# One plain gate-and-up tile less in the last half layer, its sums of x and 1/rms at earlier places, and the new keys' and values' transpositions in two shared pairs of PSUM banks

## The chip, the cores and the metric

The kernel runs on one core of one Trainium2 chip. The metric is the device time of one execution in microseconds; the time before is 1618.53 us, the median of three runs (1618.33 to 1619.42).

## The reference: what is computed

One inference step of a two-layer decoder, for a prompt of 512 tokens and 8 single sample tokens that share all weights. All is float32, the model's width is 1024 and the channel mixer's is 2816. Each layer is two half layers of SwiGLU with a token mixer between them:

```
x += 0.5 * swiglu(rms(x));  x += mixer(rms(x));  x += 0.5 * swiglu(rms(x))
swiglu(h) = (silu(h @ wg) * (h @ wu)) @ wd
rms(x) = x * rsqrt(mean(x*x) + eps) * g
```

The first layer's mixer is a causal pooling with windows of 2 to 16. The second's is sliding-window attention with sinks, over keys and values that are projected once, from x after the first layer. The outputs are the final norm's y, the last pooling rows, and the last 128 positions of keys and values for both groups.

## The kernel before

**Data and precision.** x lies as eight tiles of 128 features by 520 tokens. Each operand is split into a high and a low part (names ending in h and l), and each product is three matmuls of 260 columns (half of the 520 tokens): high with high, low x with high weight, high x with low weight. ScalarE makes a weight's high part (`wh`, L287), VectorE its low part (`wl`, L288), four k tiles at a time: a weight piece. Six buffers of wh and wl lie between these and TensorE, so ScalarE can run some six pieces ahead. SP loads the weights into three `raw` buffers.

**The half layers.** `ffn` runs four times (fi 0 to 3; the last is the second layer's second SwiGLU). The 22 gate-and-up tiles come in parts of 8, 8 and 6, and each part ends with its product with the down weights. There are two kinds of gate-and-up tile:

- `plain_tile`: gate and up over eight k tiles, for both halves of the tokens. It takes four weight pieces in the order gate, up, gate, up, and after each it runs the next entry of a list of *hooks*. VectorE's L751 and L753 then read the gate's and the up's bank pair, with ScalarE's silu (L752) between.
- `strassen_tile`: the same result with seven products of half size, from sums of weight blocks and sums of x. It takes seven pieces. Of the sums of weights, VectorE makes two (L221, L227), POOL one inside raw (L214), and one comes from two loads into a buffer `S`, the second an accumulating one by POOL (L398). It evacuates more: ScalarE's L775, L780, L783, L791, VectorE's L787 to L798.

The first `NPL[fi]` tiles of a half layer are plain, since the sums of x and 1/rms (`R`) aren't there yet; the hooks make them. Before, `NPL` is 4, 3, 2, 3.

**Sums of x and 1/rms.** `sums` is a generator of eight steps. For each of four pairs of x tiles, ScalarE makes `xa` and `xb` (L863, two buffers in all); VectorE makes t1 (L868) and t2 (L869) in a first step, t3 (L873) and t4 (L874) in a second; each step ends with a split of its tile into th (ScalarE, L379) and tl (VectorE, L380). 1/rms is three parts: TensorE adds up the squares (L560), VectorE takes a chain of small operations (L564 to L574, then L1912), and `rstd_all` has TensorE transpose the result (L586, L587) into a bank pair from which ScalarE copies it to R (L588, L589). Each plain tile's evacuation waits for R.

**PSUM.** Outside attention the eight banks are four pairs (`duo`, names ps_ with a number). A plain tile takes one pair for the gate and one for the up half; 1/rms holds one until R is copied.

**New keys and values.** The third `ffn` begins with `outputs` among its hooks, in its first plain tile. It transposes the new keys kT and values vT from features to tokens on TensorE (L1375, L1376, L1391, L1398), ScalarE copies the banks to `win`, `knew`, `vtok` and `vnew`, and POOL's queue stores them.

**Order.** A scheduler puts the instructions of each engine in an order when the kernel is built, from the order of the code, the buffers that are free and its estimates; only operations marked `later` keep the order of the code. On the chip each engine takes its row strictly in turn.

Of the kernel before, what the change touches and what calls it, by code (L numbers as in the profile page):

```python
# [11 lines left out]
F32 = mybir.dt.float32  # L12
# [16 lines left out]
NH = 3  # L29

FIRST = 264
NPL = (4, 3, 2, 3)
PIN0 = 6
SEVEN = {(f, p) for f in range(4) for p in (0, 1)}
HD = 64
# [289 lines left out]
def yoco_step(ctx, tc, ins, outs):  # L325
# [622 lines left out]
    def deferred(n, tmp, tag, tags, lst, w=TOK):  # L948

        def f(k):  # L950
            z = pair(tags, [P, w])
            split(tuple(a[:, :TOK] for a in z), x[k], gcol(n, k))
            lst.append(z)
            square(k, tmp, tag)

        return f
# [44 lines left out]
    def start_hooks(tmp, n, tt, late, norm_tok=rstd_tok):  # L1001

        steps = sums(tmp, n, tt)
        step = lambda: next(steps, None)
        there[0] = False
        none = lambda: None

        def norm():
            norm_tok()
            step()  # L1010

        def norm_all():
            rstd_all()
            known()

        return [none] * late + [norm, step, norm_all] + [step] * 6


    mov1 = []
    with ff_pool() as tmp:  # L1020
# [131 lines left out]
                    yield  # L1152

        after = delayed(1, tmp, "g", XX, mov1, TW)
        ffn(0, tmp, mov0, start_hooks(tmp, 0, tt, 2), tt, HH, after, pool_prep(), first, hold=True)

    with tc.tile_pool(name="pm", bufs=2, reuse_waits="tile") as pm:
        for k in range(KT):
# [129 lines left out]
    with ff_pool() as tmp:  # L1288

        later(nc.sync.dma_start(pool_sample[0, :, 0:14, :], state_pool[0, :, 1:15, :]))  # L1290
        for dst, src in ((k_win_s, cache_k), (v_win_s, cache_v)):
            later(
                nc.sync.dma_start(
                    dst[:, 0:127].rearrange("b s g d -> b s (g d)"), src[:, 1:128].rearrange("b s g d -> b s (g d)")
                )
            )
        later(nc.sync.dma_start(sraw, attn_sinks.broadcast_to([P, 16])))
        for b in range(NS):
            later(nc.sync.dma_start(sink_s[b * 16 : (b + 1) * 16, 0:1], attn_sinks.rearrange("l h -> h l")))
        tt = {}  # L1300
        ffn(1, tmp, mov2, start_hooks(tmp, 2, tt, 2), tt, HH, deferred(N_KV, tmp, "g", XX, movk))


    kvp = ctx.enter_context(tc.tile_pool(name="kvp", bufs=1, space=bass.MemoryType.DRAM))
# [17 lines left out]
    with ff_pool() as tmp:  # L1322

        s4 = sinks.rearrange("p (g i b e) -> p g i b e", g=2, i=4, b=4)
        sr = sraw.rearrange("p (g e i) -> p g i e", g=2, e=2)
        for b in range(4):
            for g in range(2):
                V.tensor_copy(s4[:, g, :, b, :], sr[:, g])
        V.tensor_scalar(nsinks, sinks, -1.0, None, op0=ALU.mult)
        V.tensor_scalar(sink_s[:, 1:2], sink_s[:, 0:1], -1.0, None, op0=ALU.mult)  # L1330
        cs = rawp.tile([P, 2, TOK], F32, tag="raw", name="cs")
        nc.scalar.dma_start(cs.rearrange("p a t -> p (a t)"), consts[:, C_COS : C_COS + 2 * TOK])

        def kv_pass(after):
            banks = [duo() for _ in range(2)]
            for k0 in (0, 4):
                ws = [W.get(), W.get()]
                W.prefetch()
                for k in range(k0, k0 + 4):
                    for w, bk in zip(ws, banks):  # L1340
                        mm(w, k - k0, movk[k], bk, k == 0, k == KT - 1)
                    after(k)
            return banks

        def during_k(k):
            if k == 1:
                rstd_tok()
            if k == 3:
                rstd_all()

        mov3, tt = [], {}
        steps = sums(tmp, 3, tt)

        def during_v(k):
            mov3.append(pair(HH, [P, TOK]))
            split(mov3[k], x[k], gcol(3, k))
            if k >= 4:
                next(steps)

        kb = kv_pass(during_k)  # L1360
        for i in range(2):
            V.tensor_tensor(cs[:, i, :], cs[:, i, :], R, op=ALU.mult)
        kT = [tmp.tile([P, TOK], F32, tag="ph", name="kT", bufs=3) for g in range(2)]
        for g in range(2):
            rope(kT[g], kb[g], cs[:, 0, :], cs[:, 1, :], tmp, ("g", "t"))
        vb = kv_pass(during_v)
        vT = [tmp.tile([P, TOK], F32, tag="g", name="vT") for g in range(2)]
        for g in range(2):
            V.tensor_tensor(halves(vT[g]), vb[g][:, :, :H], halves(R), op=ALU.mult)

        def outputs():
            win = tmp.tile([P, 256], F32, tag="t", name="win")
            pk = ps()
            for g in range(2):
                T.transpose(pk[:, g * P : (g + 1) * P], kT[g][:, 384:512], ident)  # L1375
                T.transpose(pk[:NS, 256 + g * P : 256 + (g + 1) * P], kT[g][:, SP:], ident)  # L1376
            S.copy(win, pk[:, :256])
            knew = tmp.tile([NS, 256], F32, tag="sb", name="knew", bufs=2)
            vnew = tmp.tile([NS, 256], F32, tag="sb", name="vnew", bufs=2)
            S.copy(knew, pk[:NS, 256:512])  # L1380
            nc.gpsimd.dma_start(k_win_p[0].rearrange("s g d -> s (g d)"), win)
            nc.gpsimd.dma_start(k_win_s[:, 127].rearrange("b g d -> b (g d)"), knew)
            nc.gpsimd.dma_start(k_new, knew)
            for g in range(2):
                nc.gpsimd.dma_start(kT_kept[g], kT[g][:, :SP])
            for b2 in range(2):
                pv = ps()
                for b in (2 * b2, 2 * b2 + 1):
                    for g in range(2):
                        o = (b % 2) * 256 + g * P  # L1390
                        T.transpose(pv[:, o : o + P], vT[g][:, b * P : (b + 1) * P], ident)  # L1391
                vtok = tmp.tile([P, 2, 256], F32, tag="pl", name="vtok", bufs=3)
                S.copy(vtok, pv.rearrange("p (b c) -> p b c", b=2))
                nc.gpsimd.dma_start(v_kept[b2], vtok)
            nc.gpsimd.dma_start(v_win_p[0].rearrange("s g d -> s (g d)"), vtok[:, 1, :])
            pvs = ps()
            for g in range(2):
                T.transpose(pvs[:NS, g * P : (g + 1) * P], vT[g][:, SP:], ident)  # L1398
            S.copy(vnew, pvs[:NS, :256])
            nc.gpsimd.dma_start(v_win_s[:, 127].rearrange("b g d -> b (g d)"), vnew)  # L1400
            nc.gpsimd.dma_start(v_new, vnew)

        kc, kk, vv = [], [], []

        def attention_prep():


            for i in range(4):
                kc.append(splp.tile([P, 2, 256], F32, tag="S", name="kc", bufs=4))
                later(nc.sync.dma_start(kc[i], cache_k[2 * i : 2 * i + 2].rearrange("b s g d -> s b (g d)")))  # L1410
                nc.gpsimd.dma_start(kc[i][0:1], k_new[2 * i : 2 * i + 2, :])
            kept = []
            for i in range(4):
                kept.append(tmp.tile([P, SP], F32, tag="ph" if i < 2 else "pl", name="kept", bufs=3))
                src = kT_kept[i] if i < 2 else v_kept[i - 2].rearrange("p b c -> p (b c)")
                later(nc.sync.dma_start(kept[i], src))
            yield
            for i in range(4):
                z = pair(("tl", "tl"), [P, SP])
                if i < 2:  # L1420
                    kk.append(z)
                    split(z, kept[i])
                else:
                    vv.append(tuple(a.rearrange("p (b c) -> p b c", b=2) for a in z))
                    split(vv[-1], kept[i].rearrange("p (b c) -> p b c", b=2))
                if i:
                    yield
            for i in range(4):
                pk = ps()
                for j in range(4):  # L1430
                    T.transpose(pk[:, j * P : (j + 1) * P], kc[i][:, j // 2, (j % 2) * P : (j % 2 + 1) * P], ident)
                S.copy(kc[i].rearrange("p b c -> p (b c)"), pk)
                yield

        step = lambda: next(steps, None)
        hooks = [step, outputs] + [step] * 4
        ffn(2, tmp, mov3, hooks, tt, XX, deferred(4, tmp, "g", HH, mov4), attention_prep())
# [410 lines left out]
    with ff_pool() as tmp:  # L1848
# [61 lines left out]
        def norm_tok():  # L1910
            rstd_tok((0, P, 2 * P, 3 * P, 400, A.start, L.start))
            later(V.tensor_scalar(rh, r_tok[:, 5:7], -0.5, None, op0=ALU.mult))  # L1912
# [141 lines left out]
            store(3, 0)  # L2054
            ordered[0] = False

        ffn(3, tmp, mov6, start_hooks(tmp, 5, tt, 1, norm_tok), tt, HH, final_after, by_parts=tail)


# [29 lines left out]
```

## Time and profile before

| | |
|---|---|
| runs, median (lowest to highest) | 1618.53 us (1618.33 to 1619.42) |
| the profiled execution | 1619.61 us, its span 1617.8 us |
| busy of the span | PE 99%, PEld 98%, DVE 87%, ACT 60%, POOL 19% |
| granted TensorE clock | 0.997 |
| matmul records | 13350 |
| DMA | 254.64 MB, mean 157 GB/s |

Places are given in microseconds from the span's start. The transpositions of new keys and values lie at 771 to 775, the last half layer's plain tiles from 1258 to 1295. In a timeline's row stand the start, the duration, the engine, the line, the operation, output and inputs, shapes, how many were merged, and in square brackets how long the engine idled before it and what ended that. Instructions on an engine overlap, so the time that one costs in a full queue is the distance between starts and not its duration.

### The profile page before, as it was taken

The page shows a single profiled execution, that of the slowest core. Times are in us where ns is not written, and L with a number is a line of the kernel's source. Part 1 is how long each engine was busy: PE and PEld are TensorE (multiplying, and loading weights), DVE is VectorE, ACT ScalarE, POOL GpSimd, SP SyncE. Part 2 cuts the span into 40 slices and gives each one's busy share as a digit, 9 for nine tenths or more (in the row PEclk, how much of TensorE's full clock was granted, in tenths as well). Part 3 has the DMA queues.
Part 4 walks back from the last instruction along what each step waited for, and adds up shares of the span by engine and source line. Part 5 has one row for each costly group of instructions (what it writes and reads, how often), then busy time and mean ns, then how long its engine had stood idle before and what let it go on. Part 6 is the DMA issues. An engine that isn't in the chain of part 4 may idle for free.

```text
span 1617.8 us, 35069 instructions
## 1 busy us (share of the span) xinstructions
PE 1602.7 (99%) x13350; PEld 1591.9 (98%) x13350; DVE 1415.0 (87%) x2775; ACT 974.7 (60%) x2024; POOL 308.1 (19%) x346
## 2 busy tenths in 40 slices
PE   9999999999999999999999999999999999999997
PEld 9999999999999999999999999999999999999997
DVE  6999999879999999978899999877787989999876
ACT  6765665657665665655565565655786665565555
POOL 1122122101121222100322212200461112222200
PEclk9999999999999999999999999999999999999999
DMA  9588888754687888744788878852333668888841
GB/s 238 114 183 189 179 177 189 172 161 126 129 184 173 186 185 181 156 130 112 192 179 177 190 172 182 183 164 81 72 79 83 140 139 182 183 183 183 189 123 54
DMA packets 418837, 254.64 MB, mean 157 GB/s; under 512 B 13134, under 2 KB 399174, under 8 KB 418628
## 3 DMA queue, kind: packets, MB, share of 16 engines
q1 hardware_dynamic: 339390, 187.30, 41.8%
q0 software_dynamic: 75520, 60.00, 25.8%
q10 hardware_dynamic: 3758, 5.09, 1.0%
q8 instruction: 105, 1.72, 0.4%
q14 instruction: 64, 0.52, 0.1%
HBM read 218.07 MB, written 6.11 MB: 139 GB/s over the span
## 4 chain that ended last, share of the span: by engine, by line
PE 98%; ACT 1%; DVE 1%; DMA 0%; issue 0%; POOL 0%; SPq 0%; DVEq 0%; ACTq 0%; POOLq 0%
PE ps L632 67%; PE ps L604 23%; PE pv L1611 1%; PE pv L1186 1%; PE pv L1584 1%; PE pv L1231 1%; PE ps L1526 1%; PE ps L1963 0%; PE ps L1970 0%; DMA raw<-in_ffn_w_gate_dram 0%; PE ps L560 0%; ACT wh L287 0%; PE pv L1717 0%; PE ps L1067 0%; PE ps L1873 0%
## 5 line engine op out<-in xcount | busy, mean ns | idle before, releaser
L287 ACT ACTIVATE wh<-raw 128x512 fp32r<-128x512 f32 (+1 forms) x768 | 448.7, 619 | 270.1 <-PE ps L632 80.8
L288 DVE TENSOR_TENSOR wl<-raw,wh 128x512 fp32r<-128x512 f32 (+1 forms) x768 | 500.2, 675 | 62.2 <-ACT wh L287 60.9
L632 PE MATMUL ps<-th,wh 128*128 128x260 f32 x1216 | 342.9, 283 | 0.4 <-ACT sb L780 0.4
L632 PE MATMUL ps<-tl,wh 128*128 128x260 f32 x1216 | 342.7, 283 | 0.0
L632 PE MATMUL ps<-th,wl 128*128 128x260 f32 x1216 | 341.6, 282 | 0.0
L632 PE MATMUL ps<-xh,wh 128*128 128x260 f32 x896 | 252.1, 283 | 0.8 <-ACT wh L287 0.7
L632 PE MATMUL ps<-xl,wh 128*128 128x260 f32 x896 | 251.3, 282 | 0.0
L632 PE MATMUL ps<-xh,wl 128*128 128x260 f32 x896 | 250.6, 282 | 0.0
L632 PEld LDWEIGHTS ps<-th,wh 128*128 128x128 f32 x1216 | 228.8, 188 | 1.1 <-ACT sb L780 0.6
L632 PEld LDWEIGHTS ps<-tl,wh 128*128 128x128 f32 x1216 | 228.8, 188 | 0.0
L632 PEld LDWEIGHTS ps<-th,wl 128*128 128x128 f32 x1216 | 228.3, 188 | 0.0
L398 POOL DMA_DIRECT2D S<-in_ffn_w_up_dram x76 | 101.2, 1331 | 465.5 <-DMA S<-in_ffn_w_up_dram 143.0
L632 PE MATMUL ps<-hh,wh 128*128 128x260 f32 x656 | 184.0, 284 | 1.6 <-ACT wh L287 0.7
L632 PE MATMUL ps<-hl,wh 128*128 128x260 f32 x656 | 184.0, 283 | 0.0
L632 PE MATMUL ps<-hh,wl 128*128 128x260 f32 x656 | 183.2, 282 | 0.0
L214 POOL DMA_DIRECT2D raw<-raw x108 | 95.4, 884 | 430.3 <-DVE wl L288 168.5
L632 PEld LDWEIGHTS ps<-xh,wh 128*128 128x128 f32 x896 | 168.1, 188 | 1.6 <-ACT wh L287 1.6
L632 PEld LDWEIGHTS ps<-xl,wh 128*128 128x128 f32 x896 | 168.4, 188 | 0.0
L632 PEld LDWEIGHTS ps<-xh,wl 128*128 128x128 f32 x896 | 168.1, 188 | 0.0
L632 PEld LDWEIGHTS ps<-hh,wh 128*128 128x128 f32 x656 | 123.0, 188 | 2.7 <-ACT wh L287 1.1
L632 PEld LDWEIGHTS ps<-hl,wh 128*128 128x128 f32 x656 | 123.2, 188 | 0.1
L632 PEld LDWEIGHTS ps<-hh,wl 128*128 128x128 f32 x656 | 122.9, 188 | 0.0
(369 smaller groups left out, 3673.7 us busy)
## 6 DMA issues: line engine op xcount, KB each, us to landing
raw<-in_ffn_w_gate_dram SPq DMA_DIRECT2D x87, 512.0 KB, 4.4
raw<-in_ffn_w_up_dram SPq DMA_DIRECT2D x87, 512.0 KB, 6.0
raw<-in_ffn_w_down_dram SPq DMA_DIRECT2D x128, 256.0 KB, 4.8
raw<-raw POOLq DMA_DIRECT2D x108, 256.0 KB, 3.9
S<-in_ffn_w_up_dram SPq DMA_DIRECT2D x76, 256.0 KB, 3.3
S<-in_ffn_w_up_dram POOLq DMA_DIRECT2D x76, 256.0 KB, 5.4
raw<-in_ffn_w_down_dram SPq DMA_DIRECT2D x16, 768.0 KB, 5.0
S<-in_ffn_w_down_dram SPq DMA_DIRECT2D x32, 256.0 KB, 3.1
```

The costliest lines, as they stand in the source:

```text
L214: G.dma_start(blk(raw, 2, 1), blk(raw, 1, 1), accum_op=ALU.add)
L287: pin(nc.scalar.activation(dh, src, AF.Copy))
L288: pin(nc.vector.tensor_tensor(dl, src, dh.bitcast(F32), op=ALU.subtract))
L398: return [ld(lambda t: t, a), lambda t: nc.gpsimd.dma_start(t, b, accum_op=ALU.add)]
L604: ins = T.matmul(banks[:, hf, :H], a[:, kk, :], hcols(b, hf), start=(first and i == 0), stop=(last and i == 2),)
L632: T.matmul(bank[:, :H], a[:, kk, :], b, start=(not more and kk == 0 and i == 0), stop=(kk == 3 and i == 2), skip_group_check=more,)
L1186: later(T.matmul(o, a[:, c], b[:, kk, :], start=(n == 0), stop=(n == 5)))
L1231: later(T.matmul(o, zz[tau][z][:, c], b, start=(i == 0), stop=(i == len(lst) - 1)))
L1526: later(T.matmul(o, q_[rows, qc], k_[rows, kc_], start=(i == 0), stop=(i == 2)))
L1584: later(T.transpose(self.both[bi][:, kt * 256 + e * P : kt * 256 + (e + 1) * P], z, ident))
L1611: later(T.matmul(o, a, p_[:, kc_], start=(n == 0), stop=(n == 3 * len(kts) - 1)))
```

## The change

Three edits.

- The last half layer has two plain tiles instead of three, so its third tile is the first of the seven-product kind.
- Hooks are written as words, one for each weight piece of a plain tile: `s` a step of the sums, `n` the squares' sums with the small chain, `a` R and what waits for it, `-` nothing. For the first two half layers the words give the list that they had. In the last one, two steps now stand at the first piece (before: nothing), one at the second with 1/rms as before, three at the third (before: one), R at the fourth as before, and the last three within the second plain tile (before: six, over the second and third).
- In `outputs`, two bank pairs are taken at once, and all transpositions of keys and values are written first; the copies follow. Before, four pairs were taken in turn, each with its transpositions and copies.

```diff
-NPL = (4, 3, 2, 3)
+NPL = (4, 3, 2, 2)
...
-        def norm():
-            norm_tok()
-            step()
+        norm0 = norm_tok
...
-        return [none] * late + [norm, step, norm_all] + [step] * 6
+        kinds = {"-": none, "s": step, "n": norm0, "a": norm_all}
+
+        def many(word):
+            def f():
+                for c in word:
+                    kinds[c]()
+
+            return f
+
+        return [many(w) for w in late.split()]
...
-        ffn(1, tmp, mov2, start_hooks(tmp, 2, tt, 2), tt, HH, deferred(N_KV, tmp, "g", XX, movk))
+        ffn(1, tmp, mov2, start_hooks(tmp, 2, tt, "- - ns s a s s s s s s"), tt, HH, deferred(N_KV, tmp, "g", XX, movk))
...
-            pk = ps()
+            two = [duo(), duo()]
+            pk, pvs = two[0][:, 0, :], two[1][:, 1, :]
+            pv = [two[0][:, 1, :], two[1][:, 0, :]]
             for g in range(2):
                 T.transpose(pk[:, g * P : (g + 1) * P], kT[g][:, 384:512], ident)
                 T.transpose(pk[:NS, 256 + g * P : 256 + (g + 1) * P], kT[g][:, SP:], ident)
+            for b in range(4):
+                for g in range(2):
+                    o = (b % 2) * 256 + g * P
+                    T.transpose(pv[b // 2][:, o : o + P], vT[g][:, b * P : (b + 1) * P], ident)
+            for g in range(2):
+                T.transpose(pvs[:NS, g * P : (g + 1) * P], vT[g][:, SP:], ident)
             S.copy(win, pk[:, :256])
...
             for b2 in range(2):
-                pv = ps()
-                for b in (2 * b2, 2 * b2 + 1):
-                    for g in range(2):
-                        o = (b % 2) * 256 + g * P
-                        T.transpose(pv[:, o : o + P], vT[g][:, b * P : (b + 1) * P], ident)
                 vtok = tmp.tile([P, 2, 256], F32, tag="pl", name="vtok", bufs=3)
-                S.copy(vtok, pv.rearrange("p (b c) -> p b c", b=2))
+                S.copy(vtok, pv[b2].rearrange("p (b c) -> p b c", b=2))
...
-            pvs = ps()
-            for g in range(2):
-                T.transpose(pvs[:NS, g * P : (g + 1) * P], vT[g][:, SP:], ident)
...
-        ffn(3, tmp, mov6, start_hooks(tmp, 5, tt, 1, norm_tok), tt, HH, final_after, by_parts=tail)
+        ffn(3, tmp, mov6, start_hooks(tmp, 5, tt, "ss ns sss a ss s", norm_tok), tt, HH, final_after, by_parts=tail)
```

The engines' rows differ at two places only: where the keys and values are transposed, and in the last half layer's first part. In the rows below, the changed kernel's line numbers are 7 to 11 higher behind the edited helper; a name in square brackets is the engine whose semaphore a row waits for.

**TensorE at the transpositions**, in the third half layer's first plain tile. ps_10785 and ps_10786 are that tile's gate and up pairs; ps_10986 (before) and ps_10984 (changed) are the next tile's gate pair. Before:

```order
L1375 MATMUL ps_10856<-ident,kT 128x128 [waits DVE_49]
L1376 MATMUL ps_10856<-ident,kT 8x128
L1391 MATMUL ps_10870<-ident,vT 128x128 x4
L1375 MATMUL ps_10856<-ident,kT 128x128 [waits DVE_49]
L1376 MATMUL ps_10856<-ident,kT 8x128
L604 MATMUL ps_10786<-hh,wl 128x260
L1391 MATMUL ps_10878<-ident,vT 128x128 [waits Activation_49]
L1391 MATMUL ps_10878<-ident,vT 128x128 x3
L1398 MATMUL ps_10887<-ident,vT 8x128 [waits PE_49,Activation_49]
L1398 MATMUL ps_10887<-ident,vT 8x128
L604 MATMUL ps_10986<-hh,wh 128x260 [waits Activation_49]
```

Changed:

```order
L1386 MATMUL ps_10858<-ident,kT 128x128 [waits DVE_49]
L1387 MATMUL ps_10858<-ident,kT 8x128
L1391 MATMUL ps_10859<-ident,vT 128x128 x4
L1386 MATMUL ps_10858<-ident,kT 128x128 [waits DVE_49]
L1387 MATMUL ps_10858<-ident,kT 8x128
L1391 MATMUL ps_10858<-ident,vT 128x128 x4
L1393 MATMUL ps_10859<-ident,vT 8x128 x2
L604 MATMUL ps_10786<-hh,wl 128x260
L604 MATMUL ps_10984<-hh,wh 128x260 [waits DVE_49]
```

All transpositions stand ahead of the up half's last matmul, none behind a wait for ScalarE, and the next tile's first row waits for VectorE in place of ScalarE.

**VectorE at the same place**: t_10966 and t_10967 (t_10964 and t_10965) are the last pair of sums, raw_10523 a weight buffer. Before:

```order
L868 TENSOR_TENSOR t_10966<-xa 128x260
L869 SCALAR_TENSOR_TENSOR t_10966<-t_10966,xb 128x260
L288 TENSOR_TENSOR wl<-raw_10523,wh 128x512
L873 TENSOR_TENSOR t_10967<-xb,xa 128x260
L874 SCALAR_TENSOR_TENSOR t_10967<-t_10966,xb 128x260
L227 TENSOR_TENSOR raw_10523<-raw_10523 128x512
L751 TENSOR_TENSOR g<-ps_10785,R 128x520
```

Changed:

```order
L868 TENSOR_TENSOR t_10964<-xa 128x260
L751 TENSOR_TENSOR g<-ps_10785,R 128x520
L869 SCALAR_TENSOR_TENSOR t_10964<-t_10964,xb 128x260
L288 TENSOR_TENSOR wl<-raw_10523,wh 128x512
L873 TENSOR_TENSOR t_10965<-xb,xa 128x260
```

The read of the gate's pair (L751) moves ahead of five operations.

**ScalarE in the last half layer's second plain tile**, around the splits of the third tile's weights (raw_17745, and raw_17746 in the changed kernel) up to R. Before:

```order
L287 ACTIVATE wh<-raw_17745 128x512 x2
L863 ACTIVATE xa<-x_82,gT 128x520
L379 ACTIVATE th<-t_17993 128x520
L379 ACTIVATE th<-t_17994 128x520
L863 ACTIVATE xb<-x_86,gT 128x520
L588 COPY R<-ps_17967 128x512
L589 COPY R<-ps_17967 128x8
```

Changed:

```order
L863 ACTIVATE xa<-x_82,gT 128x520
L863 ACTIVATE xb<-x_86,gT 128x520
L287 ACTIVATE wh<-raw_17746 128x512 x2
L863 ACTIVATE xa<-x_83,gT 128x520
L379 ACTIVATE th<-t_18013 128x520
L379 ACTIVATE th<-t_18014 128x520
L863 ACTIVATE xb<-x_87,gT 128x520
L588 COPY R<-ps_17987 128x512
L589 COPY R<-ps_17987 128x8
```

R stands behind the third pair's xa and xb, where before it stood behind the second's.

**TensorE there, changed**: ps_17987 is the pair that R comes from, ps_18127 and ps_18128 the second plain tile's gate and up pairs.

```order
L604 MATMUL ps_18127<-xl,wh 128x260 x2
L586 MATMUL ps_17987<-ident,r_tok 128x128 [waits DVE_49]
L586 MATMUL ps_17987<-ident,r_tok 128x128 x3
L587 MATMUL ps_17987<-ident,r_tok 128x8
L604 MATMUL ps_18127<-xh,wl 128x260 x2
L604 MATMUL ps_18127<-xh,wh 128x260 x2
L604 MATMUL ps_18127<-xl,wh 128x260 x2
L604 MATMUL ps_18127<-xh,wl 128x260 x2
L604 MATMUL ps_18128<-xh,wh 128x260 [waits PE_49,Activation_49]
```

Before:

```order
L604 MATMUL ps_18089<-xl,wh 128x260 x2
L604 MATMUL ps_18089<-xh,wl 128x260 x2
L586 MATMUL ps_17967<-ident,r_tok 128x128 [waits DVE_49]
L586 MATMUL ps_17967<-ident,r_tok 128x128 x3
L587 MATMUL ps_17967<-ident,r_tok 128x8
L604 MATMUL ps_18089<-xh,wh 128x260 x2
```

The transpositions of 1/rms stand 40 matmuls into the second tile, before 12, and eight ahead of the first row of the up pair, which waits for ScalarE's copies.

More of the change, by code (lines that the diff above doesn't have):

```diff
@@ L1154, in yoco_step @@
         after = delayed(1, tmp, "g", XX, mov1, TW)
-        ffn(0, tmp, mov0, start_hooks(tmp, 0, tt, 2), tt, HH, after, pool_prep(), first, hold=True)
+        ffn(0, tmp, mov0, start_hooks(tmp, 0, tt, "- - ns s a s s s s s s"), tt, HH, after, pool_prep(), first, hold=True)
     with tc.tile_pool(name="pm", bufs=2, reuse_waits="tile") as pm:
@@ L1372, in outputs @@
             win = tmp.tile([P, 256], F32, tag="t", name="win")
-            pk = ps()
+            knew = tmp.tile([NS, 256], F32, tag="sb", name="knew", bufs=2)
+            vnew = tmp.tile([NS, 256], F32, tag="sb", name="vnew", bufs=2)
+            two = [duo(), duo()]
+            pk, pvs = two[0][:, 0, :], two[1][:, 1, :]
+            pv = [two[0][:, 1, :], two[1][:, 0, :]]
             for g in range(2):
@@ L1376, in outputs @@
                 T.transpose(pk[:NS, 256 + g * P : 256 + (g + 1) * P], kT[g][:, SP:], ident)
+            for b in range(4):
[4 more added lines that the diff above has]
+                T.transpose(pvs[:NS, g * P : (g + 1) * P], vT[g][:, SP:], ident)
             S.copy(win, pk[:, :256])
-            knew = tmp.tile([NS, 256], F32, tag="sb", name="knew", bufs=2)
-            vnew = tmp.tile([NS, 256], F32, tag="sb", name="vnew", bufs=2)
             S.copy(knew, pk[:NS, 256:512])
```

## Prediction

> **What bounds the kernel now.** I read the page's busy times first, then the chain of work that ended last, then TensorE's waits, then the timelines of the two places that the diff touches. From the page, busy time by engine, and the chain's shares:
>
> ```profile
> PE 1602.7 (99%) x13350; PEld 1591.9 (98%) x13350; DVE 1415.0 (87%) x2775; ACT 974.7 (60%) x2024; POOL 308.1 (19%) x346
> PE 98%; ACT 1%; DVE 1%; DMA 0%; issue 0%; POOL 0%; SPq 0%; DVEq 0%; ACTq 0%; POOLq 0%
> ```
>
> TensorE is busy 1602.7 of 1617.8 us. Time can only come from two sources: fewer matmuls, or the 15 us in which TensorE stands. Its waits (waiter, releaser: us in total, times, longest) put two of these in the new keys' and values' transpositions:
>
> ```profile
> PE ps L604 <- ACT vtok L1393: 0.6, 1, 0.6
> PE ps L1391 <- ACT vtok L1393: 0.5, 1, 0.5
> ```
>
> In the last half layer's first 48 us the engines' busy times by stretch are (length, then PE, PEld, DVE, ACT, POOL, granted clock, DMA share, GB/s):
>
> ```profile
> 1258.00:1270.00 12.00, 12.00 (x104) 12.00 (x103) 10.28 (x23) 7.53 (x13) 0.00 (x0) 1.00 0.54 121
> 1270.00:1282.00 12.00, 12.00 (x102) 12.00 (x102) 10.36 (x23) 9.17 (x17) 4.37 (x4) 1.00 1.08 210
> 1282.00:1294.00 12.00, 12.00 (x103) 12.00 (x102) 11.79 (x25) 7.82 (x14) 1.99 (x3) 1.00 0.56 132
> 1294.00:1306.00 12.00, 12.00 (x101) 12.00 (x101) 9.30 (x17) 7.33 (x15) 1.32 (x1) 1.00 0.39 109
> ```
>
> TensorE never stands here, at full clock. VectorE is the next engine: 41.73 of 48 us, so 6.3 us to spare.
>
> **Term 1: one tile of the last half layer.** A plain tile is 2 banks x 8 k x 3 terms x 2 halves = 96 matmuls of 260 columns; a seven-product tile is 7 x 4 x 3 = 84. So 12 go. Their pace, from two pieces of the chain (start, us, what):
>
> ```profile
> 1273.43 21.64 PE ps L604 x180
> 1295.07 76.81 PE ps L632 x640
> ```
>
> 21.64 / 180 = 0.1202 and 76.81 / 640 = 0.1200 us for one, so 12 x 0.120 = **-1.44 us**, all on the path, since TensorE has no gap there. The Trainium skill, "TensorE: Matmul & The Clock Gate", section "Back-to-back issue gap", gives N / 2.4 + 2.5 ns, which is an estimate of 111 ns for 260 columns and would make the term -1.33; the rows' 120 ns is taken.
>
> What else the tile brings: three more weight pieces to split (ScalarE, then VectorE), two sums of weight blocks and more evacuation on VectorE, and one more S load on SP, its accumulating load on POOL and POOL's add inside raw. The prices on VectorE and the pace of its queue:
>
> ```profile
> 1265.27 1.89 DVE L288 TENSOR_TENSOR wl<-raw,wh 128x512 fp32r<-128x512 f32 x3
> 1267.42 0.17 DVE L564 TENSOR_SCALAR nv<-ps 128x7 f32<-128x7 f32 x1 [0.27 <-PE ps L560]
> 1267.62 0.17 DVE L565 TENSOR_SCALAR ny<-nv 128x7 int32<-128x7 int32 x1
> 1270.31 0.42 DVE L868 TENSOR_TENSOR t<-xa 128x260 f32<-128x260 f32 x1
> 1270.64 0.42 DVE L873 TENSOR_TENSOR t<-xb,xa 128x260 f32<-128x260 f32 x1
> ```
>
> Successive starts give about 0.6 us for 512 or 520 columns, 0.34 for 260, and 0.1 to 0.2 for the small ones of 1/rms (0.2 where each waits for the one before). The exchange adds 3 + 2 pieces at 0.6 = 3.0 and evacuations (L787, L790 and three halves, 2.24, for L751 and L753, 1.22) of 1.0: 4.0 us more on VectorE, in 1.44 us less time. Its cover is the 6.3 us above, nearly used up. POOL and the queues have room: POOL works 7.68 of the 48 us. In the first stretch the DMA share is 0.54. The S load now stands ahead of the third tile's raw load, which SP issues at about 1248 (third row below), and what VectorE adds from it is due some 20 us later:
>
> ```profile
> S<-in_ffn_w_up_dram SPq DMA_DIRECT2D x76, 256.0 KB, 3.3
> S<-in_ffn_w_up_dram POOLq DMA_DIRECT2D x76, 256.0 KB, 5.4
> 1248.49 0.37 SPq L394 DMA_DIRECT2D raw<-in_ffn_w_gate_dram  x1
> ```
>
> 3.3 + 5.4 us to landing lie well inside that: cost nothing.
>
> **Term 2: 1/rms behind the sums.** The sums now stand between the steps of 1/rms on VectorE, and ScalarE's copies to R stand behind the third xb. From the timelines and, for L560, the chain: where TensorE begins the first plain tile, its rows that make R, and ScalarE's copies, before:
>
> ```profile
> 1258.23 0.40 PE L604 MATMUL ps<-xh,wh 128*128 128x260 f32 x2
> 1265.93 1.46 PE ps L560 x14
> 1272.71 0.60 PE L586 MATMUL ps<-ident,r_tok 128*128 128x128 f32 x4
> 1274.18 0.59 ACT L588 COPY R<-ps 128x512 f32<-128x512 f32 x1
> 1274.66 0.17 ACT L589 COPY R<-ps 128x8 f32<-128x8 f32 x1
> ```
>
> In the changed order the transpositions for R come after 40 of the second tile's matmuls instead of 12. They start at 1258.23 + 136 x 0.120 + 1.46 = 1276.0, end 0.58 later, and 8 matmuls on, at 1277.55, the second tile's up bank wants the pair of banks that R is copied from. Now VectorE, from 1265.27 to the L874 that the last th and xb ahead of R on ScalarE wait for: ten operations of 0.6, eight of 0.34, eleven small ones of together about 1.5, and 0.3 for waits on ScalarE: 10.5, so 1275.8. r_tok is ready two microseconds earlier, ahead of L586. Then on ScalarE, by successive starts here and in term 3's rows, th (773.47 to 774.01, 0.54), xb (0.62), R (0.48), and R's last 8 columns (0.17): 1277.7 with the hand-over. TensorE stands 1277.7 - 1277.55, **about +0.2 us**. Ends: 0 if VectorE is 0.2 quicker, 1.2 if the chain of nine hand-overs between the engines adds 1 us more; 0.2 is the walk's own value.
>
> The tail of the sums: TensorE ends the second plain tile at 1277.7 + 48 x 0.120 = 1283.5, and the first seven-product tile begins with 36 matmuls of x, then 14 of the next tile's, before the third 12 want the T sums' first half, at 1289.5. VectorE has written the last of these by 1286.9 and all sums by 1290.0 by the same walk (the second half is wanted about 1296). Nearest call: the low part of the next tile's first piece, nine operations (4.2 us) behind the L753 that waits for that tile's end at 1283.5: ready 1287.8, wanted 40 matmuls after 1283.5, 1288.3. Slack 0.5, so I put 0 there, with 0.5 as its other end.
>
> **Term 3: the transpositions.** TensorE, ScalarE and VectorE there, before (start, us, engine, line):
>
> ```profile
> 771.45 0.27 PE L1375 MATMUL ps<-ident,kT 128*128 128x128 f32 x1
> 771.67 0.60 PE L1391 MATMUL ps<-ident,vT 128*128 128x128 f32 x4
> 772.10 0.27 PE L1375 MATMUL ps<-ident,kT 128*128 128x128 f32 x1
> 773.10 0.66 PE L1391 MATMUL ps<-ident,vT 128*128 128x128 f32 x4 [0.49 <-ACT vtok L1393]
> 774.62 0.51 PE L604 MATMUL ps<-hh,wh 128*128 128x260 f32 x2 [0.62 <-ACT vtok L1393]
> ...
> 771.34 0.71 ACT L863 ACTIVATE xb<-x,gT 128x520 f32<-128x520 f32 x1
> 771.96 0.61 ACT L287 ACTIVATE wh<-raw 128x512 fp32r<-128x512 f32 x1
> 772.48 0.56 ACT L1393 COPY vtok<-ps 128x512 f32<-128x512 f32 x1
> 772.95 0.37 ACT L1377 COPY win<-ps 128x256 f32<-128x256 f32 x1
> 773.21 0.36 ACT L1380 COPY knew<-ps 8x256 f32<-8x256 f32 x1
> 773.47 0.63 ACT L379 ACTIVATE th<-t 128x520 fp32r<-128x520 f32 x1
> 774.01 0.56 ACT L1393 COPY vtok<-ps 128x512 f32<-128x512 f32 x1
> ...
> 772.00 0.42 DVE L868 TENSOR_TENSOR t<-xa 128x260 f32<-128x260 f32 x1
> 774.75 0.69 DVE L751 TENSOR_TENSOR g<-ps,R 128x520 f32<-128x520 f32 x1
> ```
>
> Before, TensorE stands until the second vtok is copied, at 774.57, behind an xa, an xb, a wh and a th in ScalarE's queue. After, all 14 transpositions go to two pairs of banks without a wait between. Four of them take 772.10 - 771.67 = 0.43, so 14 take 1.50: with the last matmul (0.12) TensorE is through at 771.45 + 1.62 = 773.07. The next tile's first matmul then waits for VectorE, not ScalarE: it takes the bank pair of the gate half just finished, which L751 frees. In the new order L751 stands right behind the L868 of 772.00: it starts at 772.34 and ends at 773.03. TensorE goes on at about 773.1 instead of 774.62: **-1.5 us**. Ends: -1.6 (no wait at all) and -0.3 (if both shared pairs had to be copied first: 772.48 + 0.47 x 2 + 0.26 x 3 = 774.2). ScalarE's copies, now 1.7 us in one stretch to 774.2, are late only for the next up bank, wanted 24 matmuls after 773.1, 776.0; that is also the cost if the cover goes: nothing until they slip 1.8 us. POOL's add inside raw now stands behind two more issues of values:
>
> ```profile
> 779.63 0.89 POOL L214 DMA_DIRECT2D raw<-raw  x1 [1.20 <-DVE wl L288]
> 781.10 0.55 POOL L1400 DMA_DIRECT2D out_dram<-vnew  x1 [0.58 <-DMA S<-in_ffn_w_up_dram]
> ```
>
> Two such issues (1.1) fit into the 1.20 that it waited, so nothing behind it moves.
>
> **Sum.** -1.44 + 0.2 - 1.5 = -2.7. On the profiled execution's 1619.61 us (span 1617.8 and 1.8 around it) this is 1616.9; that execution lies 1.1 over the median of the runs, so on 1618.53 it is **1615.8**. A measurement of this kernel tells about 0.2%, 3.2 us, from no change (1615.3 to 1621.8), so my forecast is a real gain that stays just inside it.
>
> **Rivals.**
> 1. A wait takes the removed one's place: the next tile waits for ScalarE's copies out of the shared pairs. Term 3 is then -0.3 and the time 1617.0. The order speaks against it (that row waits on VectorE). 8%.
> 2. ScalarE's R comes 1.2 us late: 1616.8. For it: nine hand-overs and ScalarE's 9.17 of 12 us in that stretch. 14%.
> 3. More than the sum: both small losses are 0 and some of TensorE's other stands, 13 us in all, shrink with the new phase. Two of 0.7 or so going would give 1614.5. Nothing in the rows says that they would. 13%.
> 4. Transpositions that don't overlap: 14 x 0.27 = 3.8, TensorE goes on at 775.3 and term 3 is +0.7: 1618.0. The rows' 0.43 for four is against it. 1%. The Trainium skill's page named above, section "Part 4: PE-mode transpose", reports about 275 ns each in a kernel's context; by that rule this would be the result, and the trace disagrees as to pace, though each one's duration is 0.27.
> 5. Slower: VectorE becomes the bound of the first seven-product tiles. Place: the T sums and splits before the first of them. Point: when its queue is more than 2.6 us behind my walk (1289.5 - 1286.9). At worst none of the 6.3 us of cover is usable and TensorE waits for the whole exchange, +4.0 + 1.44: terms 1 and 2 become +4.0 and the time 1621.0; with rival 1 on top, 1622.2. Against: in the last stretch above VectorE idles 2.7 us, so it catches up by itself. 7%.
>
> The forecast holds 57%. The range is 1614.7 to 1618.0: the forecast with the ends of terms 2 and 3, rivals 1, 2 and 4, and part of 3, leaving out rival 5 and the far part of 3. Faster by over 0.2% needs another 0.5 us: most of rival 3 and an eighth of the forecast, 0.20; slower by over 0.2% is the far half of rival 5, 0.04; within, 0.76.
>
> **What would show it.** Between the transpositions TensorE has no wait, and the next L604 starts 1.6 us after the first of them, released by L751. TensorE's count falls by 12 and its pace stays 0.120. A wait of 0 to 0.5 us for ScalarE's R copy stands in the second plain tile, and none at the first seven-product tile. I am wrong if the gate tile waits on a win, knew or vtok copy, if T rows stand as releasers of TensorE, or if VectorE is still gapless after the fourth tile.

## The result, and the profile after

The changed kernel takes **1616.37 us** (median of 22 runs, 1615.54 to 1617.31) against 1618.74 (22 runs, 1617.54 to 1620.48): ratio 0.9985, 95% interval 0.9979 to 0.9991. That is a real gain of about 2.4 us and within 0.2%, the case that the prediction held likeliest (1615.8, range 1614.7 to 1618.0). Its profiled execution took 1616.43 us, span 1614.7.

Busy time by engine, from the page of the changed kernel:

```profile
PE 1599.9 (99%) x13338; PEld 1589.5 (98%) x13338; DVE 1417.0 (88%) x2783; ACT 976.4 (60%) x2030; POOL 310.0 (19%) x348
```

TensorE has 13338 matmuls in place of 13350: the 12 of term 1. Of the two waits for `vtok` nothing is left; TensorE's waits in the changed kernel show one row in their place:

```profile
PE ps L604 <- DVE g L751: 0.6, 1, 0.6
```

The transpositions in the changed kernel's timeline (start, us, engine, line; the lines are 7 to 11 higher than before):

```profile
772.01 0.27 PE L1386 MATMUL ps<-ident,kT 128*128 128x128 f32 x1
...
772.23 0.60 PE L1391 MATMUL ps<-ident,vT 128*128 128x128 f32 x4
...
772.56 0.42 DVE L868 TENSOR_TENSOR t<-xa 128x260 f32<-128x260 f32 x1
...
773.32 0.38 PE L1393 MATMUL ps<-ident,vT 128*8 128x128 f32 x2
...
773.46 0.36 PE L604 MATMUL ps<-hh,wl 128*128 128x260 f32 x1
773.52 0.37 ACT L1394 COPY win<-ps 128x256 f32<-128x256 f32 x1 [0.38 <-PE ps L1391]
773.63 0.70 DVE L751 TENSOR_TENSOR g<-ps,R 128x520 f32<-128x520 f32 x1 [0.65 <-PE ps L1393]
...
774.38 0.51 PE L604 MATMUL ps<-hh,wh 128*128 128x260 f32 x2 [0.56 <-DVE g L751]
```

All 14 transpositions and the up half's last matmul run without a wait, to 773.61. Then TensorE stands until 774.38, for L751, and L751 had itself waited 0.65 us for **TensorE's L1393**, a transposition of the new values. From the first transposition to the next tile's first matmul it is 2.37 us; before it was 774.62 - 771.45 = 3.17. The place gained 0.80 us, not 1.5.

The last half layer, in pieces of the chain from the squares' sum (L560) to the stand for `wh`. Before, of which the prediction showed a part:

```profile
1265.93 1.46 PE ps L560 x14
...
1474.00 0.62 ACT wh L287
```

and changed:

```profile
1264.05 1.46 PE ps L560 x14
...
1274.89 7.04 PE ps L604 x56
1281.93 86.84 PE ps L632 x724
...
1470.89 0.62 ACT wh L287
```

208.07 us became 206.84: **-1.23 us**, where terms 1 and 2 said -1.44 + 0.2. From the second plain tile's end on, 724 matmuls run in one piece at 0.120 us, with no stand at the first seven-product tile. The engines' busy times in the same stretches, with the columns of the prediction (PE, PEld, DVE, ACT, POOL, granted clock, DMA share, GB/s):

```profile
1258.00:1270.00 12.00, 12.00 (x104) 12.00 (x103) 10.93 (x25) 8.48 (x15) 0.53 (x1) 1.00 0.70 159
1270.00:1282.00 12.00, 12.00 (x101) 11.81 (x100) 11.21 (x26) 8.97 (x18) 2.67 (x4) 1.00 0.67 125
1282.00:1294.00 12.00, 12.00 (x102) 12.00 (x101) 12.00 (x24) 8.85 (x19) 2.29 (x3) 1.00 0.49 131
1294.00:1306.00 12.00, 12.00 (x103) 12.00 (x102) 11.05 (x23) 7.15 (x15) 2.22 (x2) 1.00 0.84 169
```

VectorE works 45.19 of the 48 us in place of 41.73, and for 12 us without a gap. TensorE does not wait for it.

The two profiled executions are 3.1 us apart in span. -0.80 and -1.23 are the change. -1.57 is a stretch in attention in which before's execution had TensorE at half clock and the changed kernel's had not (last section), and the changed kernel began its first products 0.56 us later. These four make -3.04, and 0.1 is not placed. So the change itself is worth **about 2.0 us** by the profiles; what the medians show beyond that, 0.3 us, has no place in them.

### The profile page after: what moved, and what is told of

Its sections match the earlier page's. It is cut to its first block, busy times and chain, and to the rows that moved or that the text cites. A ratio compares the mean times of both kernels' runs of the same rounds, so it can differ in the third digit from the quotient of the medians.

```text
span 1614.7 us, 35073 instructions
## 1 busy us (share of the span) xinstructions
PE 1599.9 (99%) x13338; PEld 1589.5 (98%) x13338; DVE 1417.0 (88%) x2783; ACT 976.4 (60%) x2030; POOL 310.0 (19%) x348
## 4 chain that ended last, share of the span: by engine, by line
PE 98%; DVE 1%; ACT 0%; POOL 0%; issue 0%; DVEq 0%; ACTq 0%; POOLq 0%
PE ps L632 68%; PE ps L604 23%; PE pv L1618 1%; PE pv L1193 1%; PE pv L1591 1%; PE pv L1238 1%; PE ps L1533 1%; PE ps L1970 0%; PE ps L1977 0%; PE ps L1065 0%; PE ps L560 0%; PE pv L1724 0%; PE ps L1074 0%; ACT wh L287 0%; PE ps L1880 0%; PE pv L1678 0%
## 5 line engine op out<-in xcount | busy, mean ns | idle before, releaser
L632 PE MATMUL ps<-th,wh 128*128 128x260 f32 x1232 | 347.3, 283 | 0.4 <-ACT sb L780 0.4
L632 PE MATMUL ps<-tl,wh 128*128 128x260 f32 x1232 | 347.1, 283 | 0.0
L632 PE MATMUL ps<-th,wl 128*128 128x260 f32 x1232 | 345.8, 282 | 0.0
L632 PE MATMUL ps<-xh,wh 128*128 128x260 f32 x908 | 255.4, 283 | 0.8 <-ACT wh L287 0.7
L632 PE MATMUL ps<-xl,wh 128*128 128x260 f32 x908 | 254.6, 282 | 0.0
L632 PE MATMUL ps<-xh,wl 128*128 128x260 f32 x908 | 254.2, 282 | 0.0
```

What stands on the lines that cost most here:

```text
L632: T.matmul(bank[:, :H], a[:, kk, :], b, start=(not more and kk == 0 and i == 0), stop=(kk == 3 and i == 2), skip_group_check=more,)
```

## The experiments

Two theories of the missing 0.7 us were put against each other. W: L751 writes `g` into the buffer that vT's first half had (`g` and `vT` share the tag "g", two buffers), so it cannot start before the last transposition that reads that half. S: ScalarE's copies out of the shared pairs hold the next tile, the prediction's rival 1. For the rest the question was what the exchange of the tile and the new hook words are each worth, and how far VectorE was from rival 5.

**1. The transpositions alone** (the kernel before with the third edit).

> The kernel before with the third edit alone: all transpositions first, into two shared pairs. Theory W (VectorE's L751 writes g into the buffer that vT's first half had, so it cannot start before the last transposition of that half, which now stands 13th of 14): from the first transposition to the next tile's first matmul 2.4 us, where the kernel before has 3.2 and the prediction's walk gave 1.6; TensorE's one wait there is for L751, 0.6 us; time -0.8 us against the kernel before. Rival A (the place is worth the -1.5 that was predicted, and the 0.8 comes from something that the other edits do): 1.6 us there and -1.5. Rival S (ScalarE's copies out of the shared pairs hold the next tile): TensorE's wait there is released by an L1387 to L1399 copy, 2.9 us and -0.3.

1617.67 us (11 runs), ratio to before 0.9993 (0.9985 to 1.0002). The place takes 2.37 us, as in the changed kernel and as W said; TensorE's wait there is for L751 and not for a copy, against S, and the place is not worth 1.5, against A. L1386 here is what L1393 is in the changed kernel:

```profile
771.53 0.27 PE L1379 MATMUL ps<-ident,kT 128*128 128x128 f32 x1
...
772.84 0.38 PE L1386 MATMUL ps<-ident,vT 128*8 128x128 f32 x2
...
773.15 0.70 DVE L751 TENSOR_TENSOR g<-ps,R 128x520 f32<-128x520 f32 x1 [0.64 <-PE ps L1386]
...
773.90 0.51 PE L604 MATMUL ps<-hh,wh 128*128 128x260 f32 x2 [0.56 <-DVE g L751]
```

In pieces of the chain, from the squares' sum ahead of the place to the first seven-product tile it is 38.58 us, against 39.38 before and 38.58 in the changed kernel. So -0.80 belongs to this edit alone, and the last half layer keeps its time (208.17 us). The whole time can't tell this gain from none; the place can.

**2. The tile and the hook words alone** (the changed kernel with `outputs` as before).

> The changed kernel with the transpositions as they were: the exchanged tile and the new hook words alone. 12 matmuls fewer. From L560 in the last half layer to the next stand of TensorE -1.2 us against the kernel before (208.07 us there): -1.44 for the matmuls and +0.15 to +0.2 for R's copy. The key and value place has its 3.2 us of before. Time -1.2 us by this theory. Rival V (VectorE, that works without a gap for 12 us in the second plain tile, gives back more when the phase of the stage moves): a stand at the first seven-product tile, released by a th or tl row, and a time of no change or slower.

1617.64 us (11 runs), ratio 0.9995 (0.9986 to 1.0003). Last half layer 1473.07 - 1266.18 = 206.89 us, -1.18; the transpositions 3.18 us as before. No th or tl row holds TensorE, so rival V did not come. The two halves of the change add up at their places; neither median alone is clear of no change.

**3. The first half's values read sooner, VectorE's and ScalarE's rows untouched.** `later` keeps the order of the code.

```diff
-            for b in range(4):
-                for g in range(2):
+            for g in range(2):
+                for b in range(4):
                     o = (b % 2) * 256 + g * P
-                    T.transpose(pv[b // 2][:, o : o + P], vT[g][:, b * P : (b + 1) * P], ident)
-            for g in range(2):
-                T.transpose(pvs[:NS, g * P : (g + 1) * P], vT[g][:, SP:], ident)
+                    later(T.transpose(pv[b // 2][:, o : o + P], vT[g][:, b * P : (b + 1) * P], ident))
+                later(T.transpose(pvs[:NS, g * P : (g + 1) * P], vT[g][:, SP:], ident))
```

> The changed kernel with the keys first, then five transpositions of vT's first half, then five of its second; VectorE's and ScalarE's rows are the changed kernel's. The last read of vT's first half is then the 9th of the 14 transpositions in place of the 13th, with one L604 ahead of it. Theory W: L751 starts 4 x 0.109 - 0.12 = 0.3 us sooner behind the first transposition (1.3 us in place of 1.62), and the next tile's gate matmul with it (2.05 in place of 2.37). Rival P (L751's place in VectorE's row): no change, 2.37. Rival S (ScalarE's copies): they start with the last transposition as before, 2.37 or more.

1616.18 us (11 runs), ratio 0.9983 (0.9974 to 0.9992). In its timeline L1392 is the 8-column transposition that ends each half; the first one is the last read of vT's first half, and ScalarE's first copy (L1393) comes behind L751:

```profile
771.96 0.27 PE L1392 MATMUL ps<-ident,vT 128*8 128x128 f32 x1
772.07 0.60 PE L1391 MATMUL ps<-ident,vT 128*128 128x128 f32 x4
772.27 0.70 DVE L751 TENSOR_TENSOR g<-ps,R 128x520 f32<-128x520 f32 x1 [0.33 <-PE ps L1392]
...
772.48 0.37 ACT L1393 COPY win<-ps 128x256 f32<-128x256 f32 x1 [0.38 <-PE ps L1391]
772.50 0.27 PE L1392 MATMUL ps<-ident,vT 128*8 128x128 f32 x1
...
773.02 0.51 PE L604 MATMUL ps<-hh,wh 128*128 128x260 f32 x2 [0.24 <-DVE g L751]
```

L751 starts 0.31 us behind the start of that read. In the changed kernel it is 773.63 - 773.32 = 0.31 too. The place (770.96 to 773.02) takes 2.06 us in place of 2.37, as W said. S falls: TensorE goes on at 773.02, when ScalarE has still most of its copies to do.

**4. Values ahead of keys, the first half first.** In `outputs`, vT's ten transpositions are written ahead of kT's four, those of the first half first, without `later`.

> The changed kernel with the values' transpositions written ahead of the keys', those of vT's first half ahead of those of its second. Theory W: vT's first half is read early, L751 follows long before TensorE ends the up half, and the next tile's gate matmul does not wait: from TensorE's last L604 of the tile to the next tile's first less than 0.2 us, where the changed kernel has 0.77; -0.75 us there against the changed kernel, -2.8 against the kernel before if TensorE does not stand for vT itself, which it now asks for some 4 us sooner. Rival S: the wait stays, released by ScalarE's copies, at 0.7 or more. Rival P (L751 only waits for its place in VectorE's row): nothing changes, 0.77.

1615.90 us (11 runs), ratio 0.9982 (0.9973 to 0.9991): the lowest median of all, though not clear of the changed kernel's. The scheduler now spreads the transpositions among the up half's last 17 matmuls. In the timeline L1388 and L1389 read vT, L1391 and L1392 read kT, and the last row is the next tile's first matmul:

```profile
771.84 0.27 PE L1389 MATMUL ps<-ident,vT 128*8 128x128 f32 x1
...
772.15 0.70 DVE L751 TENSOR_TENSOR g<-ps,R 128x520 f32<-128x520 f32 x1 [0.61 <-PE ps L1389]
...
773.90 0.40 PE L604 MATMUL ps<-hh,wh 128*128 128x260 f32 x2
```

Again 0.31 us from the last read to L751 (771.84 to 772.15), but now L751 is done by 772.85, while TensorE still works on the up half, to 773.9, and no wait is left. The scheduler also moved L751 and other operations in VectorE's row here; experiment 3, with that row unchanged, is the cleaner test of the cause. From the squares' sum ahead of the place to the first seven-product tile it is 37.78 us: -0.80 against the changed kernel, -1.60 against before. So the place could give what term 3 promised; one buffer's reads had to stand in another order.

**5. The old hook places with two plain tiles.**

```diff
-        ffn(3, tmp, mov6, start_hooks(tmp, 5, tt, "ss ns sss a ss s", norm_tok), tt, HH, final_after, by_parts=tail)
+        ffn(3, tmp, mov6, start_hooks(tmp, 5, tt, "- ns s a s s s s s s", norm_tok), tt, HH, final_after, by_parts=tail)
```

> The changed kernel with two plain tiles in the last half layer but the hooks' old places: 1/rms first, then the sums, the last two of the eight steps behind the second plain tile. Theory N (the new words are needed): the last pair of sums then comes when TensorE already works on the first seven-product tile; TensorE stands there for a th or tl row (T rows as releasers), 0.5 to 3 us, and loses most of the 1.23 that the tile saved. Theory C (VectorE's order of the sums matters little, since the sums are wanted only from 50 matmuls after the second plain tile on): no stand there, R's copy 1 us sooner, and the time of the changed kernel within 0.2 us.

1623.95 us (7 runs), ratio 1.0028 (1.0017 to 1.0040): **7.6 us slower than the changed kernel**, more than N's upper end. TensorE at the first seven-product tile:

```profile
1287.97 0.29 PE L632 MATMUL ps<-th,wl 128*128 128x260 f32 x1
1291.98 0.39 PE L632 MATMUL ps<-th,wh 128*128 128x260 f32 x1 [3.72 <-ACT th L379]
1292.72 0.58 PE L632 MATMUL ps<-tl,wh 128*128 128x260 f32 x1 [0.35 <-DVE tl L380]
1293.10 0.42 PE L632 MATMUL ps<-th,wl 128*128 128x260 f32 x1
1293.99 0.59 PE L632 MATMUL ps<-th,wh 128*128 128x260 f32 x1 [0.47 <-ACT sa L775]
```

This is rival 5's mechanism: the last pair's sums are late, and TensorE stands 4.5 us for th, tl and what hangs on them. The last half layer takes 1478.45 - 1263.72 = 214.73 us, 7.89 more than the changed kernel's. What goes beyond these stands, 3.35 us, is mostly the clock behind them (last section). With the old words the exchange of the tile would have cost some 6 us (5.1 by the medians, with the 0.8 of the transpositions in it).

**6. The new hook words with three plain tiles** (`NPL` back to 4, 3, 2, 3).

> The changed kernel with its hook words, but three plain tiles in the last half layer as before: the earlier sums alone, without the tile. From L560 to TensorE's stand in the last half layer 208.1 us, the same as before (within 0.2: only R's copy may come late); -0.8 us against the kernel before, all of it from the transpositions. Rival: the earlier sums take a stand out of a later place by themselves; then less than 207.8 there.

1618.17 us (11 runs), ratio 0.9996 (0.9987 to 1.0005). Last half layer 1472.71 - 1264.63 = 208.08 us, before 208.07. The words alone give nothing and cost nothing; they only make the exchange possible.

**7. The first pair of sums one piece later** (words "- nsss ss a ss s").

> The changed kernel with the first two steps of the sums at the second piece, behind 1/rms, in place of the first piece (words -, nsss, ss, a, ss, s); the rest as in the changed kernel. It asks how far the sums may slip. In the changed kernel the low part of the fourth pair's first sum ends at 1285.23 us and its first matmul starts at 1288.52: 3.3 us of slack. With the old words that low part came 7.8 us later behind L560 and TensorE stood 4.5 us. Theory Q (only the place in VectorE's queue counts): one pair of sums is four times 0.34 and twice 0.6, 2.6 us, less than the slack; no stand for a th or tl row, 206.9 us from L560 to TensorE's stand in the last half layer, the changed kernel's time within 0.3 us. Rival L (what counts is that the sums fill the waits between the small steps of 1/rms, which then stand bare again): the slip is 4 us or more, TensorE stands 0.5 to 2 us for th, and the half-clock stretch seen behind the 3.7 us stand may not come, so 0.5 to 2 us slower than the changed kernel.

1617.77 us (11 runs), ratio 0.9992 (0.9983 to 1.0001), 1.4 us slower than the changed kernel. Neither theory holds as written. No stand for a th or tl row, as Q said, and the second plain tile ends 0.26 us sooner behind L560. But the last pair's first low part ends 25.2 us behind L560 in place of 21.2, so the slip is 4.0 us and not 2.6, as L said. The last half layer takes 207.79 us, 0.95 more than the changed kernel's, and its largest new stand, 0.69 us, is for a weight, 60 us behind that low part:

```profile
1350.47 0.62 ACT wh L287
```

A likely reading is that the two engines carry the delay along, and the weights' splits behind the sums come later by it. That was not tried.

**8. One plain tile** (`NPL` 4, 3, 2, 1, words "ss nss sss as").

> The changed kernel with one plain tile in the last half layer, all eight sums and 1/rms in its four pieces (words ss, nss, sss, as). If the exchange were worth its 12 matmuls each time, another -1.44. Theory V (VectorE's cover was nearly used up by the first exchange, and this one asks for the sums 11 us sooner): TensorE stands at the first seven-product tile for th, tl or R; VectorE has 9 us of sums, 7 x 0.6 of weights and 1/rms to do in some 10 us less, so 3 to 8 us of stands; 2 to 6 us slower than the changed kernel.

1622.30 us (11 runs), ratio 1.0022 (1.0014 to 1.0031): 5.9 us slower than the changed kernel, in V's range. TensorE's stands:

```profile
1272.23 0.65 PE L586 MATMUL ps<-ident,r_tok 128*128 128x128 f32 x4 [2.13 <-DVE r_tok L574]
1274.57 0.58 PE L632 MATMUL ps<-xh,wh 128*128 128x260 f32 x1 [1.57 <-ACT R L589]
1282.94 0.39 PE L632 MATMUL ps<-th,wh 128*128 128x260 f32 x1 [1.15 <-ACT sa L775]
```

R's chain is now late as well: VectorE's cover was not enough for a second exchange. Half clock came here too (last section).

**9. The same exchange in the second half layer too** (`NPL` 4, 2, 2, 2 and the last half layer's words).

> The changed kernel with the same edit in the second half layer as well: two plain tiles in place of three, and the last half layer's words. 12 matmuls fewer again. Theory T (the saving carries over): -1.2 to -1.44 against the changed kernel. Rival V: VectorE works 56.0 of the 60 us of the stage from 370 to 430 us, against 41.7 of 48 us in the last half layer, 0.9 us idle of every 12 against 1.6, so the added 4.0 us don't fit and TensorE stands for T rows: 0.5 to 3 us slower than the changed kernel.

1620.63 us (11 runs), ratio 1.0011 (1.0002 to 1.0020): 4.3 us slower than the changed kernel, more than rival V gave. V is borne out only in part. VectorE has no gap in the second of the two stretches below, but no T row holds TensorE: it stands for R (0.74 at 410.31), then for weights' low parts (1.2, VectorE) and for ScalarE's high parts and copies (0.7), so ScalarE has a share that was not taken apart:

```profile
406.00:418.00 12.00, 10.74 (x86) 10.17 (x85) 11.00 (x32) 8.59 (x16) 1.99 (x3) 1.00 0.43 106
418.00:430.00 12.00, 10.59 (x83) 9.96 (x83) 12.00 (x24) 9.07 (x19) 0.00 (x0) 1.00 0.17 42
```

169 matmuls in 24 us, where the changed kernel has 204 there: 35 x 0.120 = 4.2 us lost for 1.44 saved, 2.8 in sum. From this half layer's squares' sum to the third's it is 348.91 us, in the changed kernel 346.26: 2.65 more. The rest of the 4.3 lies behind this stage and was not followed up.

## Why the prediction was right, and the step that failed

- **Term 1** (-1.44) holds: 12 matmuls fewer, 0.120 us each, none hidden.
- **Term 2** (+0.2) holds, by its own walk. ScalarE's copies of R in the changed kernel's timeline:

```profile
1275.22 0.59 ACT L588 COPY R<-ps 128x512 f32<-128x512 f32 x1
1275.71 0.17 ACT L589 COPY R<-ps 128x8 f32<-128x8 f32 x1
```

  and TensorE's last matmuls of the gate half with the up half's first:

```profile
1275.55 0.39 PE L604 MATMUL ps<-xh,wl 128*128 128x260 f32 x2
1275.93 0.51 PE L604 MATMUL ps<-xh,wh 128*128 128x260 f32 x2
```

  The second pair would have started 0.24 behind the first, at 1275.79; it starts at 1275.93, when R's last columns are copied: a stand of 0.14, where the walk had 1277.7 - 1277.55 = 0.15. On before's time axis (1.88 us later at L560) the start is 1277.81; the walk said 1277.7.
- **The tail of the sums at 0** holds: no th or tl row holds TensorE. The walk had all sums written by 1290.0; they end at 1287.64 + 0.69 + 1.88 = 1290.2. Its nearest call, 0.5 us of slack for the next tile's first low weight, came out at 0.4 (ready 1286.17, used 1286.58). VectorE's load (41.73 + 4.0 forecast, 45.19 measured) was right too.
- **Term 3** (-1.5) is the step that failed, measured -0.80. Its first half was right: 14 transpositions in one row, 1.45 us where the working had 1.50, no wait between them, and L751 as the releaser. Wrong was "in the new order L751 stands right behind the L868 of 772.00: it starts at 772.34 and ends at 773.03". A place in a row is not a start. L751 waits for TensorE, and not only for the gate's bank pair that it reads: it writes `g` over vT's first half, whose last read the edit had moved to the end of the transpositions. In that time frame L751 started 773.63 - 0.56 = 773.07, 0.73 late, and TensorE stood 0.77. The working knew only one condition of L751, the gate's pair, which was long met. Experiments 1, 3 and 4 show it: the same 0.31 us between that read's start and L751 in three placements, and no stand where the read comes early enough.
- **Rival 1** (ScalarE's copies) fell with experiment 3, **rival 4** (0.27 us for each transposition) with the profile after. **Rival 3** (other stands that go) did not show: no other part of the program changed by more than 0.1 us apart from the clock and the start, measured between the squares' sums along the program and to its end.
- **Rival 5** did not come, but its 7% understates how the change is built: with the sums one piece later 0.95 us of the gain is gone, with the old words all of it and 5 us more. The working priced the words as a cost (term 2); they are what holds this rival off.

Sum on the median: 1618.74 - 2.0 = 1616.7, measured 1616.37. The 0.6 us between forecast and result is term 3's error of 0.7 and the median of before, which stood 0.2 higher with more runs, less 0.3 that stays unexplained within the interval of the ratio (about 1 us either way). That the 0.3 makes up for part of term 3's error is luck.

## What to carry to other kernels

When an edit moves reads of a buffer to the end of a block, look for who writes that buffer next: with a shared tag the waiter is named by its output's buffer, not by its inputs, and a place early in an engine's row says nothing about when it may start. Before a tile is exchanged for one with fewer matmuls but more vector work, ask in which order the vector work must then come; here the order alone was worth 7.6 us and the tile 1.2. Measure small edits at their place, between two instructions that the edit doesn't touch, since the whole time scatters by more than they give.

## What the runs showed of the hardware

**Half clock without a pause.** The same columns for the kernel before, in attention, where the sixth figure is the granted clock:

```profile
1190.00:1192.00 2.00, 2.00 (x25) 1.86 (x24) 1.96 (x10) 1.39 (x5) 0.50 (x3) 1.00 0.00 0
1192.00:1193.00 1.00, 1.00 (x10) 1.00 (x10) 1.00 (x8) 1.00 (x4) 1.00 (x3) 0.89 0.00 0
1193.00:1194.00 1.00, 1.00 (x6) 1.00 (x6) 1.00 (x4) 1.00 (x5) 0.68 (x1) 0.50 0.00 0
1194.00:1195.00 1.00, 1.00 (x7) 1.00 (x6) 1.00 (x6) 0.83 (x4) 0.23 (x1) 0.50 0.00 0
1195.00:1196.00 1.00, 1.00 (x7) 1.00 (x7) 0.26 (x1) 0.37 (x1) 1.00 (x1) 0.50 0.00 0
1196.00:1198.00 2.00, 2.00 (x26) 1.83 (x28) 0.99 (x5) 1.11 (x3) 1.85 (x3) 0.95 0.05 12
```

For some 3.4 us the granted clock is 0.50, and the stretch takes 1.57 us longer than in the changed kernel's execution. Four experiments' executions (the second, sixth, seventh and ninth) had such a dip too, between 1170 and 1190; the changed kernel's and the other five had none there. Up to the last half layer the sixth's and seventh's kernels run the changed kernel's instructions in the same order on TensorE, VectorE, ScalarE and POOL, so the dip goes with the execution and not with this change. It may be why before's profiled execution lay 1.1 us over the median; how often it comes in either kernel is not known. In all eleven executions the granted clock changes only at whole multiples of 3.413 us from its first rise to full, and that first rise lies at another place in each (4.1 to 7.3 us from the start). The Trainium skill, "TensorE: Matmul & The Clock Gate", section "What's actually happening", has a free-running window of 3413 ns and half clock after an idle one; the length and the steps agree. The section "Why this matters for your kernels" asks for pauses under about 3 us to avoid it; here TensorE was busy in 9.75 of the 10 us ahead, and its longest wait in that part of attention was 0.4 us. What set it off was not settled.

**A stand that costs nearly twice its length.** The same columns for the kernel with the old words, behind its stands of 4.5 us:

```profile
1292.00:1293.00 1.00, 0.65 (x2) 0.45 (x3) 1.00 (x2) 0.00 (x0) 0.99 (x1) 0.82 0.90 234
1293.00:1299.00 6.00, 5.53 (x25) 5.23 (x26) 2.78 (x5) 2.88 (x7) 0.92 (x1) 0.50 0.63 93
1299.00:1300.00 1.00, 1.00 (x8) 1.00 (x8) 0.00 (x0) 0.57 (x2) 0.00 (x0) 0.76 0.00 0
```

The stand of 3.72 us was followed by some 6.8 us at half clock (0.36 of the first row, the second, 0.48 of the third), in which matmuls of 260 columns came every 0.216 us in place of 0.120: 25 of them in the second row, 2.4 us more. That is most of the 3.35 us by which the 7.89 us exceed the stands. Here the Trainium skill's rule on pauses over 3 us (same page, "Why this matters for your kernels") agrees. The prediction priced rival 5 by its stand alone, without the clock behind it.

No single pause of 3 us was needed in the eighth experiment: its stands of 2.13 and 1.57 us, with matmuls from 1272.23 to 1273.0 between them, were followed by 3.41 us at half clock, from 1274.59.
